# Masks and biases of attention logits: added by VectorE with the row maximum instead of by identity matmuls

## The chip, the cores and the metric

The kernel runs on one core of one Trainium2 chip. The metric is the device time of one execution in microseconds (us). Engines are named as the profile does: PE (TensorE, matmuls), PEld (its weight loads), DVE (VectorE), ACT (ScalarE), POOL (GpSimd), SP (SyncE, which issues DMAs).

## What is computed

Two transformer blocks, one after the other, on 512 tokens of width 1024, in float32. The parts that bear on the change are three attentions, each a softmax of scaled products plus a bias or a mask:

```python
def masked_softmax(logits, mask):
    logits = jnp.where(mask, logits, -jnp.inf)
    m = jnp.max(logits, axis=-1, keepdims=True)
    p = jnp.exp(logits - m)
    return p / jnp.sum(p, axis=-1, keepdims=True)
# NSA, 4 heads of 64, branches "selected" and "window": bias by distance, causal
logits_s = einsum(q_blk, kg) * scale + rel_bias[t5_bucket(dist_s)]
p_s = masked_softmax(logits_s, dist_s >= 0)
# MLA, 4 heads of 96: causal
p = masked_softmax(einsum(q_blk, k) * scale, kpos <= t0 + arange(Q_BLOCK))
# second block, grouped window attention, 8 heads: |qi - kj| <= 128, with a sink
s = jnp.where(valid, s, -jnp.inf)
m = jnp.maximum(jnp.max(s, axis=-1, keepdims=True), sk)
p = jnp.exp(s - m); p = p / (jnp.sum(p, axis=-1, keepdims=True) + jnp.exp(sk - m))
```

Around them stand projections, a compressed branch of NSA, a stick-breaking attention, a short convolution, two feed-forward nets, a gated recurrence and a cross attention to a memory.

## The kernel before

All big projections are matmuls of 128x128 weights by 512 columns, each done as three products of high and low parts (L184, L185, L186); L259 and L260 split a weight into whi (ACT) and wlo (DVE). They fill most of PE's time. The attentions work on tiles of 128 queries (NT = 4 tiles). A unit is one tile and one head (in NSA also one branch): 32 units in NSA, 16 in MLA, 32 in the window attention of the second block.

Each unit is made by `attend` in three steps. The first makes logits in a PSUM bank "L" (two of them), takes the negated row maximum (L814, DVE) and the exponential (L818, ACT, which reads the bank, takes the maximum as bias and sums the row), into an SBUF tile "sba" or "wp" (three of each). The second transposes that tile (L823, PE) and copies the result to SBUF, by ACT (L827) and DVE (L829) in turn. The third multiplies by the values (L834). `pipeline_g` runs them staggered: the second step of a unit comes two units after its first, the third three or four after. Between steps `fill` takes pieces of projection matmuls out of a list. The framework then orders each engine's queue from this program order and its own costs.

Logits are products of high and low parts: two matmuls by `mm_pair` (L879, L880) in NSA and the window attention, three (L184 to L186 with output L) in MLA. Bias and mask come on top by further matmuls into the same bank, with the identity as weights: in NSA L1124 and L1125 (high and low part of a bias table of 256 columns, tiles sbLh and sbLl, at the last 256 columns), in MLA L1337 (causal mask, 128 columns), in the window attention L1666 (upper mask at the first 128 columns, for tiles i > 0) and L1668 (causal at the last 128, for i < 3). In the window attention a `bound` lowers the negated maximum to the negated sink (L1675, DVE). NSA's compressed branch adds its bias table Tc on DVE (L1082).

The bias tables are built once: a DMA brings shifted rows, and `split` makes a high part (ACT) and a low part (DVE, L193) of their reversed columns.

Of the kernel before, what the change touches and what calls it, by code (L numbers as in the profile page):

```python
# [16 lines left out]
OP = mybir.AluOpType  # L17
# [132 lines left out]
class Kern:  # L150
# [336 lines left out]
    def setup(self):  # L487
        nc, tc, ctx, A = self.nc, self.tc, self.ctx, self.A
        self.cp = cp = ctx.enter_context(tc.tile_pool(name="cp", bufs=1))
        self.xp = ctx.enter_context(tc.tile_pool(name="xp", bufs=1))  # L490
        self.sp = ctx.enter_context(tc.tile_pool(name="sp", bufs=2))
        self.wp = ctx.enter_context(tc.tile_pool(name="wp", bufs=3))
        self.hp = ctx.enter_context(tc.tile_pool(name="hp", bufs=1))
        self.mmp = ctx.enter_context(tc.tile_pool(name="mmp", bufs=1, space=PSUM))
        self.drp = ctx.enter_context(tc.tile_pool(name="drp", bufs=1, space=DRAM))
        nc.scalar.preload_act_table_set("natural_log_exp_and_others")
        nv = A["vecs"].shape[1]
        self.vecs = self.T(cp, [P, nv], F32, "vecs")
        cm = self.T(cp, [P, P + 256], F32, "cmat")
        self.ident = cm[:, 0:P]  # L500
        self.rope = cm[:, P:P + 256].rearrange("p (t c) -> p t c", t=NT)
        self.ones = self.T(cp, [P, P], F32, "ones")
        self.mhalf = self.T(cp, [P, 12], F32, "mhalf")
        cr = self.T(cp, [P, 5 * P], F32R, "cmatr")
        nc.sync.dma_start(cm[:, :P], A["cmat"][:, :P])
        nc.vector.memset(self.ones, 1.0)
        nc.vector.memset(self.mhalf, -0.5)
        self.identr, self.trir, self.negr, self.causr, self.causupr = [cr[:, i * P:(i + 1) * P] for i in range(5)]

        def rest():  # L510
            st = self.T(self.sp, [P, 4 * P], F32, "R", 2)
            nc.sync.dma_start(st, A["cmat"][:, P:5 * P])
            nc.sync.dma_start(cm[:, P:], A["cmat"][:, 5 * P:])
            nc.vector.tensor_copy(cr[:, :P], self.ident)
            nc.vector.tensor_copy(cr[:, P:], st)

            self.lb = []
            for dr in range(2):
                l = self.T(cp, [P, 4], F32, f"lb{dr}")
                nc.vector.tensor_sub(l, self.vec(f"lb{dr}1"), self.vec(f"lb{dr}0"))  # L520
                nc.scalar.activation(l, l, AF.Exp)
                nc.vector.tensor_scalar(l, l, 1.0, None, op0=OP.add)
# [280 lines left out]
        return self.T(pool, [P, 256], F32, "junk", 1)  # L803


    def attend(self, pool, logits, nk, v, o, s, tags=("sba", "sbe", "pT"), bound=None, done=None):

        nc = self.nc
        st = {}

        def first():
            L = logits()
            nm = self.T(pool, [P, 1], F32, tags[0] + "m", 6)
            nc.vector.tensor_reduce(nm, L[:, :nk], axis=AX.X, op=OP.max, negate=True)  # L814
            if bound is not None:
                nm = bound(nm)
            p = st["p"] = self.T(pool, [P, 512], F32, tags[0], 3)
            nc.scalar.activation(p[:, :nk], L[:, :nk], AF.Exp, bias=nm, accum_out=s())  # L818
# [193 lines left out]
    def nsa_prep(self, mp, qN, kvN):  # L1012
# [17 lines left out]
        for hp in range(2):  # L1030
            Tf = self.T(mp, [P, 2, 256], F32, "sba", 3)
            nc.sync.dma_start(Tf, bass.AP(scr.tensor, scr.offset + hp * 2 * OHN + 1, [[1, P], [OHN, 2], [1, 256]]))
            tb = self.hl(mp, [P, 2, 256], "sbL", 3)
            self.split(tb, bass.AP(Tf.tensor, Tf.offset + 255, [Tf.ap[0], [256, 2], [-1, 256]]))
            TB += [tb[:, 0], tb[:, 1]]
            for i in range(NT):
                n0, n1 = max(0, 8 * i - 8), min(30, 8 * i + 6)
                s0 = n0 - (8 * i - 8)
# [4 lines left out]
                    nc.gpsimd.memset(Tc[:, i, 2 * hp:2 * hp + 2, :n0], 0.0)  # L1043
        kview = kvN[:, :, 0:256].rearrange("p t (b c) -> p t b c", b=2)[:, :, :, 0:64]
        wq = self.T(mp, [P, 1], F32, "wq8", 1)
        nc.vector.tensor_scalar(wq, self.vec("nsaq"), 0.125, None, op0=OP.mult)
        qT = []
        for c in range(2):
            self.fill(1)
# [11 lines left out]
    def nsa_units(self, mp, qts, kvN, prep, out):  # L1061
# [8 lines left out]
        def tile_units(qt):  # L1070
# [4 lines left out]
            def c_first():  # L1075
# [6 lines left out]
                nc.vector.tensor_add(lc, Lc[:, :P].rearrange("p (h n) -> p h n", n=32), Tc[:, qt])  # L1082
# [34 lines left out]
            def logits(br, h):  # L1117
                L = self.ps('L')
                self.mm_pair(L[:, :nk], h, qT, qs, kT[br], slice(0, nk))
                if qt == 0:  # L1120
                    Lb, tb = L[:, 0:P], TB[h][:, P:256]
                else:
                    Lb, tb = L[:, nk - 256:nk], TB[h]
                nc.tensor.matmul(Lb, self.identr, tb.hi, start=False, stop=True, skip_group_check=True)  # L1124
                nc.tensor.matmul(Lb, self.identr, tb.lo, start=False, stop=True, skip_group_check=True)  # L1125
                return L

            def done():
# [13 lines left out]
            for br in range(2):  # L1142
                for h in range(4):
                    vo = 64 + br * 128
                    units.append(self.attend(mp, lambda br=br, h=h: logits(br, h), nk,
                                             lambda t, vo=vo: kvN[:, t, vo:vo + 64], lambda br=br, h=h: o(br, h),
                                             lambda br=br, h=h: s(br, h), done=done if (br, h) == (1, 3) else None))
# [123 lines left out]
    def mla_proj(self, mp, ncv, cq, out):  # L1271
# [15 lines left out]
        nc.vector.tensor_scalar(wq, self.vec("mq"), 96.0 ** -0.5, None, op0=OP.mult)  # L1287
        out["mla"] = qN, kN, vN, wq

    def mla_rope(self, mp, ncv, m):  # L1290
# [34 lines left out]
    def mla_units(self, mp, hd, prep, yN):  # L1325
        nc = self.nc
        units = []

        def head(h):
            st = {}  # L1330

            def logits(qt):
# [1 line left out]
                qT, kT = hd[h]  # L1334
                L = self.ps("L")
                self.mm3(L[:, :nk], qT[:96, qt * P:nk], kT[:96, 0:nk])
                nc.tensor.matmul(L[:, nk - P:nk], self.identr, self.causr, start=False, stop=True, skip_group_check=True)  # L1337
                return L

            def o(qt):  # L1340
# [13 lines left out]
                                     rc.unsqueeze(2).to_broadcast([P, NT, 64]))  # L1354
            for qt in range(NT):
                units.append(self.attend(mp, lambda qt=qt: logits(qt), (qt + 1) * P, lambda t: prep["mla"][2][:, t, h, :],
                                         lambda qt=qt: o(qt), lambda qt=qt: s(qt), ("sba", "sbe", "pT"),
                                         done=done if qt == NT - 1 else None))
        for h in range(4):
            head(h)  # L1360
# [267 lines left out]
    def window(self, wp, qkv):  # L1628
# [15 lines left out]
        nc.vector.memset(eighth, 0.125)  # L1644
# [12 lines left out]
        def tile_units(i):  # L1657
# [4 lines left out]
            def logits(h):  # L1662
                L = self.ps('L')
                self.mm_pair(L[:, :nk], h, qT, slice(i * P, (i + 1) * P), kT[h // 4], slice(k0 * P, k1 * P))
                if i > 0:
                    nc.tensor.matmul(L[:, 0:P], self.identr, self.causupr, start=False, stop=True, skip_group_check=True)  # L1666
                if i < NT - 1:
                    nc.tensor.matmul(L[:, nk - P:nk], self.identr, self.causr, start=False, stop=True, skip_group_check=True)  # L1668
                return L

            def bound(h, m):
                if "s" not in st:
                    st["s"] = self.T(wp, [P, 8], F32, "wsum", 2)
                    st["nm"] = self.T(wp, [P, 8], F32, "wnm", 2)
                nc.vector.tensor_scalar(st["nm"][:, h:h + 1], m, nsnk[:, h:h + 1], None, op0=OP.min)  # L1675
                return st["nm"][:, h:h + 1]

            def o(h):
                if "o" not in st:
# [279 lines left out]
```

## Time and profile before

| what | us |
|---|---|
| three runs, median (lowest to highest) | 1645.45 (1644.49 to 1645.54) |
| the profiled execution, its own time | 1645.99 |
| span of its trace (1.69 lie outside) | 1644.3 |
| PE busy in the span | 1610.8 |
| DVE busy | 937.0 |
| ACT busy | 670.1 |
| POOL busy | 181.5 |

The profile is one execution. In its rows a matmul's duration runs from its start to a modelled end, and matmuls overlap, so the distance between two starts says what one takes of PE's time. [...] The first block's mixers lie before 295 us (NSA units from 138 to 240, MLA units from 255 to 290), the window attention between 950 and 1006 us.

### The profile page before, as it was taken

What the parts mean: (1) busy time and instruction counts of PE and PEld (TensorE: products, weight loads), DVE (VectorE), ACT (ScalarE), POOL (GpSimd) and SP (SyncE); (2) the same over time, 40 slices, a digit from 0 to 9 for tenths busy, and PEclk for the clock granted to TensorE, in tenths of its full rate; (3) what the DMA queues carried; (4) which work ended last, traced back from release to release, by engine and by line L of the source; (5) the groups of instructions that cost most, each with busy time, mean ns of one, the idle gap of its engine ahead of it and who ended that gap; (6) DMA issues with size and microseconds to landing.
All of it is one profiled execution on the core that took longest, in us unless ns stands there. A gap on an engine that the chain in (4) does not pass through costs nothing.

```text
span 1644.3 us, 21273 instructions
## 1 busy us (share of the span) xinstructions
PE 1610.8 (98%) x8289; PEld 1366.8 (83%) x8289; DVE 937.0 (57%) x1473; ACT 670.1 (41%) x1162; POOL 181.5 (11%) x180
## 2 busy tenths in 40 slices
PE   7999999999999999999999999999999999999998
PEld 6888888788888888878888898888888888888888
DVE  6666775644323434476766575665667556436654
ACT  4785563543222433343334354353444223223333
POOL 2121210200000001113110000330002111001110
PEclk9999999999999999999999999999999999999999
DMA  6243121133323232222222211333332333323231
GB/s 209 63 137 88 33 89 53 51 105 101 99 94 102 90 102 92 89 88 59 78 60 76 77 40 52 101 104 116 128 99 72 100 97 96 102 91 102 90 115 52
DMA packets 107976, 147.67 MB, mean 90 GB/s; under 512 B 7871, under 2 KB 58852, under 8 KB 107876
## 3 DMA queue, kind: packets, MB, share of 16 engines
q1 hardware_dynamic: 107876, 146.31, 28.3%
q8 instruction: 65, 1.06, 0.3%
q14 instruction: 35, 0.29, 0.1%
HBM read 141.79 MB, written 4.20 MB: 89 GB/s over the span
## 4 chain that ended last, share of the span: by engine, by line
PE 82%; DVE 4%; ACT 1%; DMA 1%; POOL 1%; issue 1%; SPq 0%; DVEq 0%; POOLq 0%; ACTq 0%
PE mm L184 23%; PE mm L186 23%; PE mm L185 23%; PE o L834 2%; PE lv L1560 2%; PE pT L823 1%; DVE wlo L260 1%; PE o L1603 1%; PE L L879 1%; DMA wraw<-w_down_dram 1%; PE L L880 0%; PE lv L1580 0%; POOL yq L1136 0%; DMA wraw<-w_in_dram 0%; PE L L184 0%
## 5 line engine op out<-in xcount | busy, mean ns | idle before, releaser
L260 DVE TENSOR_TENSOR wlo<-wraw,whi 128x1024 fp32r<-128x1024 f32 (+4 forms) x268 | 320.7, 1198 | 435.1 <-ACT whi L259 426.7
L259 ACT ACTIVATE whi<-wraw 128x1024 fp32r<-128x1024 f32 (+4 forms) x268 | 270.5, 1010 | 549.7 <-PE mm L185 479.8
L418 POOL TENSOR_TENSOR nacc<-nacc,nsq 128x512 f32<-128x512 f32 x30 | 46.7, 1557 | 519.6 <-ACT nsq L416 518.5
L1854 POOL TENSOR_TENSOR fz<-fz,fu 128x512 f32<-128x512 f32 x22 | 37.5, 1702 | 271.4 <-ACT fz L1853 271.4
L184 PE MATMUL mm<-H4h,whi 128*128 128x512 f32 x147 | 59.8, 407 | 0.0
L462 DVE TENSOR_TENSOR x<-mm,x 128x512 f32<-128x512 f32 x72 | 49.0, 687 | 18.7 <-PE mm L186 18.4
L184 PE MATMUL mm<-H6h,whi 128*128 128x512 f32 x147 | 58.3, 401 | 0.4 <-ACT H6h L195 0.4
L184 PE MATMUL mm<-H7h,whi 128*128 128x512 f32 x147 | 58.5, 398 | 0.0
L184 PE MATMUL mm<-H5h,whi 128*128 128x512 f32 x147 | 58.3, 396 | 0.0
L186 PE MATMUL mm<-H4h,wlo 128*128 128x512 f32 x147 | 57.5, 391 | 0.7 <-DVE wlo L260 0.7
L186 PE MATMUL mm<-H6h,wlo 128*128 128x512 f32 x147 | 57.9, 394 | 0.0
L185 PE MATMUL mm<-H6l,whi 128*128 128x512 f32 x147 | 57.8, 393 | 0.0
L186 PE MATMUL mm<-H5h,wlo 128*128 128x512 f32 x147 | 57.4, 390 | 0.0
L185 PE MATMUL mm<-H5l,whi 128*128 128x512 f32 x147 | 57.4, 390 | 0.0
L186 PE MATMUL mm<-H7h,wlo 128*128 128x512 f32 x147 | 57.4, 390 | 0.0
L185 PE MATMUL mm<-H4l,whi 128*128 128x512 f32 x147 | 57.3, 390 | 0.0
L185 PE MATMUL mm<-H7l,whi 128*128 128x512 f32 x147 | 57.3, 390 | 0.0
L184 PE MATMUL mm<-H0h,whi 128*128 128x512 f32 x139 | 55.7, 401 | 0.5 <-ACT whi L259 0.5
L184 PE MATMUL mm<-H2h,whi 128*128 128x512 f32 x139 | 55.8, 402 | 0.0
L184 PE MATMUL mm<-H3h,whi 128*128 128x512 f32 x139 | 55.7, 401 | 0.0
L184 PE MATMUL mm<-H1h,whi 128*128 128x512 f32 x139 | 55.1, 396 | 0.0
L186 PE MATMUL mm<-H3h,wlo 128*128 128x512 f32 x139 | 54.8, 394 | 0.0
(1214 smaller groups left out, 4448.5 us busy)
## 6 DMA issues: line engine op xcount, KB each, us to landing
wraw<-ffn_w_dram SPq DMA_DIRECT2D x64, 512.0 KB, 3.6
wraw<-w_up_dram SPq DMA_DIRECT2D x88, 256.0 KB, 3.1
wraw<-w_in_dram SPq DMA_DIRECT2D x36, 512.0 KB, 3.5
wraw<-w_down_dram SPq DMA_DIRECT2D x22, 512.0 KB, 3.6
wraw<-w_mem_kv_dram SPq DMA_DIRECT2D x16, 512.0 KB, 3.7
wraw<-w_in_dram SPq DMA_DIRECT2D x52, 128.0 KB, 2.3
wraw<-w_in_dram SPq DMA_DIRECT2D x20, 256.0 KB, 2.8
wraw<-cmp_w_dram SPq DMA_DIRECT2D x8, 512.0 KB, 4.2
```

Of the source, the lines that this page charges most:

```text
L184: mm(out, a.hi, b.hi, start=start, stop=False, skip_group_check=skip)
L185: mm(out, a.hi, b.lo, start=False, stop=False, skip_group_check=skip)
L186: mm(out, a.lo, b.hi, start=False, stop=stop, skip_group_check=skip)
L259: nc.scalar.activation(hi, raw, AF.Copy)
L260: nc.vector.tensor_sub(lo, raw, hi.bitcast(F32))
L418: eng.tensor_add(nm.acc, nm.acc, sq[:, :nm.N])
L462: self.nc.vector.tensor_add(self.x[k], b, self.x[k])
L823: nc.tensor.transpose(b[:, t * P:(t + 1) * P], st["p"][:, t * P:(t + 1) * P], self.ident)
L834: nc.tensor.matmul(o(), st["pT"][:, t * P:(t + 1) * P], v(t), start=(t == 0), stop=(t == nt - 1))
L879: self.nc.tensor.matmul(out, q[h][:, qs], k.hi[:, ks], start=True, stop=False)
L1560: nc.tensor.matmul(b[:, t * P:(t + 1) * P], ym[:, t * P:(t + 1) * P], mix(X, c, t * P, P), start=True, stop=True)
L1854: nc.gpsimd.tensor_mul(z, z, us[c])
```

## The change

The scale that goes into the queries changes its sign, so that the banks hold negated logits. Then one DVE instruction, `tensor_tensor_reduce`, adds a table of negated biases or masks, writes the sum to the SBUF tile and takes the minimum of the row, starting from a value `least` (the negated sink in the window attention, 3.0e38 elsewhere). ACT's exponential reads that SBUF tile with scale -1, in place. The identity matmuls go, and with them the 32 minima L1675. The tables are as wide as the longest row of logits: four tiles of 512 columns in NSA (256 of them zero), one in MLA, one of 384 in the window attention.

```diff
+        cn = self.T(cp, [P, 2 * P], F32, "cmask2")
...
+            nc.vector.tensor_scalar(cn, st[:, 2 * P:], -1.0, None, op0=OP.mult)
...
             L = logits()
-            nm = self.T(pool, [P, 1], F32, tags[0] + "m", 6)
-            nc.vector.tensor_reduce(nm, L[:, :nk], axis=AX.X, op=OP.max, negate=True)
-            if bound is not None:
-                nm = bound(nm)
+            nm, least = bound() if bound is not None else (self.T(pool, [P, 1], F32, tags[0] + "m", 6), 3.0e38)
             p = st["p"] = self.T(pool, [P, 512], F32, tags[0], 3)
-            nc.scalar.activation(p[:, :nk], L[:, :nk], AF.Exp, bias=nm, accum_out=s())
+            nc.vector.tensor_tensor_reduce(p[:, :nk], L[:, :nk], bias, 1.0, least, op0=OP.add, op1=OP.min, accum_out=nm)
+            nc.scalar.activation(p[:, :nk], p[:, :nk], AF.Exp, bias=nm, scale=-1.0, accum_out=s())
...
-            tb = self.hl(mp, [P, 2, 256], "sbL", 3)
-            self.split(tb, bass.AP(Tf.tensor, Tf.offset + 255, [Tf.ap[0], [256, 2], [-1, 256]]))
-            TB += [tb[:, 0], tb[:, 1]]
+            for a, tg in enumerate(("sbLh", "sbLl")):
+                tb = self.T(mp, [P, S], F32, tg, 3)
+                nc.gpsimd.memset(tb[:, :256], 0.0)
+                nc.scalar.activation(tb[:, 256:], bass.AP(Tf.tensor, Tf.offset + 256 * a + 255, [Tf.ap[0], [-1, 256]]),
+                                     AF.Copy, scale=-1.0)
+                TB.append(tb)
...
-        nc.vector.tensor_scalar(wq, self.vec("nsaq"), 0.125, None, op0=OP.mult)
+        nc.vector.tensor_scalar(wq, self.vec("nsaq"), -0.125, None, op0=OP.mult)
...
                 self.mm_pair(L[:, :nk], h, qT, qs, kT[br], slice(0, nk))
-                if qt == 0:
-                    Lb, tb = L[:, 0:P], TB[h][:, P:256]
-                else:
-                    Lb, tb = L[:, nk - 256:nk], TB[h]
-                nc.tensor.matmul(Lb, self.identr, tb.hi, start=False, stop=True, skip_group_check=True)
-                nc.tensor.matmul(Lb, self.identr, tb.lo, start=False, stop=True, skip_group_check=True)
                 return L
...
+        cm = self.T(mp, [P, S], F32, "sbLh", 3)
+        nc.gpsimd.memset(cm[:, :S - P], 0.0)
+        nc.gpsimd.tensor_copy(cm[:, S - P:], self.ncaus)
...
-                nc.tensor.matmul(L[:, nk - P:nk], self.identr, self.causr, start=False, stop=True, skip_group_check=True)
...
+        wb = self.T(wp, [P, 3, P], F32, "wb")
+        nc.gpsimd.tensor_copy(wb[:, 0], self.ncausup)
+        nc.gpsimd.memset(wb[:, 1], 0.0)
+        nc.gpsimd.tensor_copy(wb[:, 2], self.ncaus)
...
-                if i > 0:
-                    nc.tensor.matmul(L[:, 0:P], self.identr, self.causupr, start=False, stop=True, skip_group_check=True)
-                if i < NT - 1:
-                    nc.tensor.matmul(L[:, nk - P:nk], self.identr, self.causr, start=False, stop=True, skip_group_check=True)
...
-                nc.vector.tensor_scalar(st["nm"][:, h:h + 1], m, nsnk[:, h:h + 1], None, op0=OP.min)
-                return st["nm"][:, h:h + 1]
+                return st["nm"][:, h:h + 1], nsnk[:, h:h + 1]
```

Left out of it: the compressed branch subtracts in place of adding, the MLA and window queries get the same change of sign, and the identity is no longer cast for PE.

PE's queue in the window attention, one unit of the second tile, before (L is the bank of logits, pT and o those of the transposes and of the output; wk and wq are keys and queries, cmatr the constant matrices):

```order
L879 MATMUL L_8189<-wk1h_7899,wq2h_7862 128x384
L880 MATMUL L_8189<-wk1l_7900,wq2h_7862 128x384
L1666 MATMUL L_8189<-cmatr_80 128x128
L1668 MATMUL L_8189<-cmatr_80 128x128
L823 MATMUL pT_8202<-cmat_77,wp_8130 128x128 x3
L834 MATMUL o_8182<-qkv_6001,wpT_8180 128x64 x3
```

The same place in the changed kernel, where mm is the bank of a projection:

```order
L881 MATMUL L_8081<-wk1h_7831,wq2h_7794 128x384
L882 MATMUL L_8081<-wk1l_7832,wq2h_7794 128x384
L186 MATMUL mm_8270<-H2h_5482,wlo_8275 128x512
L881 MATMUL L_8102<-wk1h_7831,wq2l_7797 128x384
L882 MATMUL L_8102<-wk1l_7832,wq2l_7797 128x384
L825 MATMUL pT_8068<-cmat_77,wp_8008 128x128 x3
L836 MATMUL o_8074<-qkv_5929,wpT_8035 128x64 x3
L184 MATMUL mm_8270<-H3h_5496,whi_8274 128x512
L185 MATMUL mm_8270<-H3l_5497,whi_8274 128x512
L825 MATMUL pT_8090<-cmat_77,wp_8025 128x128 x3
L836 MATMUL o_8074<-qkv_5929,wpT_8072 128x64 x3
```

The rows L1666 and L1668 are gone, and pieces of a projection (L184 to L186), which before stood elsewhere in the queue, now stand between the units.

DVE's queue in the NSA units beside the MLA preparation (mss, mrr2t and mrr2u belong to that preparation, wlo to a weight), before:

```order
L814 TENSOR_REDUCE sbam_2393<-L_2388 128x1
L210 TENSOR_SCALAR mrr2t_2309<-mss_527_2283 128x32
L814 TENSOR_REDUCE sbam_2414<-L_2409 128x1
L196 SCALAR_TENSOR_TENSOR mla_t_2794<-yT_445_1996,vecs_76,mla_p_2793 128x512
L217 TENSOR_TENSOR mrr2u_2311<-mrr_536_2308 128x32
L196 SCALAR_TENSOR_TENSOR mla_t_2796<-yT_447_2003,vecs_76,mla_p_2795 128x512
L218 TENSOR_TENSOR mrr2u_2311<-mrr2u_2311,mrr2t_2309 128x32
L814 TENSOR_REDUCE sbam_2435<-L_2430 128x1
```

And in the changed kernel, where the two rows L819 are one `tensor_tensor_reduce`, and the second of them only writes the row's minimum:

```order
L831 COPY sbe_2333<-pT_2329 128x384
L210 TENSOR_SCALAR mrr2t_2274<-mss_528_2248 128x32
L260 TENSOR_TENSOR wlo_2344<-wraw_2342,whi_2343 128x512
L819 ISA sba_2355,sbam_2354<-L_2351,sbLl_1289 128x384
L819 ISA sbam_2354 128x1
L819 ISA sba_2374,sbam_2373<-L_2370,sbLh_1300 128x384
L819 ISA sbam_2373 128x1
L217 TENSOR_TENSOR mrr2u_2276<-mrr_537_2273 128x32
L260 TENSOR_TENSOR wlo_2398<-wraw_2396,whi_2397 128x512
```

Each maximum L814 has become two rows, of which the first also reads a bias table (sbLh, sbLl) and writes the tile sba.

## Rows read from the trace of the kernel before

**Rows 1.** page, busy time of each engine and the chain that ended last
```profile
PE 1610.8 (98%) x8289; PEld 1366.8 (83%) x8289; DVE 937.0 (57%) x1473; ACT 670.1 (41%) x1162; POOL 181.5 (11%) x180
PE 82%; DVE 4%; ACT 1%; DMA 1%; POOL 1%; issue 1%; SPq 0%; DVEq 0%; POOLq 0%; ACTq 0%
```

**Rows 2.** by stage: stretch, length, busy PE, PEld, DVE, ACT, POOL (instructions), clock, DMA
```profile
138.00:180.00 42.00, 39.81 (x239) 33.36 (x238) 23.09 (x67) 19.62 (x69) 4.95 (x5) 1.00 0.14 40
180.00:217.00 37.00, 36.03 (x236) 31.79 (x234) 35.30 (x103) 24.09 (x64) 5.28 (x8) 1.00 0.20 58
255.00:290.00 35.00, 34.12 (x222) 30.16 (x220) 20.86 (x42) 15.58 (x44) 1.02 (x2) 1.00 0.20 61
966.00:990.00 24.00, 24.00 (x202) 23.78 (x201) 16.61 (x46) 14.13 (x42) 0.00 (x0) 1.00 0.01 2
```

**Rows 3.** lines L1124 and L1668: count, shortest/median/longest ns, first and last start
```profile
L1124 PE MATMUL L<-sbLh,cmatr x32: 274/279/415, 140.5 to 238.4; 128*128 128x256 f32 x24, 128*128 128x128 f32 x8
L1668 PE MATMUL L<-cmatr x24: 221/276/279, 952.9 to 987.3; 128*128 128x128 f32 x24
```

**Rows 4.** timeline of PE in an NSA unit: start us, us, engine, line, tiles
```profile
174.02 0.28 PE L1124 MATMUL L<-sbLh,cmatr 128*128 128x256 f32 x1
174.14 0.28 PE L1125 MATMUL L<-sbLl,cmatr 128*128 128x256 f32 x1
```

**Rows 5.** by stage, 180 to 217: first L1124 (PE, PEld), then L814 (DVE) alone
```profile
180.00:217.00 37.00, 2.88 (x10) 1.88 (x10) 1.00 0.20 58
180.00:217.00 37.00, 5.84 (x11) 1.00 0.20 58
```

**Rows 6.** timeline of PE in two MLA units
```profile
260.23 0.23 PE L1337 MATMUL L<-cmatr 128*128 128x128 f32 x1
260.29 0.38 PE L823 MATMUL pT<-cmat,sba 128*128 128x128 f32 x2
261.50 0.27 PE L1337 MATMUL L<-cmatr 128*128 128x128 f32 x1
261.61 0.48 PE L184 MATMUL mm<-mla_p,whi 128*128 128x512 f32 x1
```

**Rows 7.** timeline of all engines in one unit of the window attention
```profile
976.35 0.23 PE L1666 MATMUL L<-cmatr 128*128 128x128 f32 x1
976.41 0.28 PE L1668 MATMUL L<-cmatr 128*128 128x128 f32 x1
976.52 0.52 PE L823 MATMUL pT<-cmat,wp 128*128 128x128 f32 x3
976.72 0.56 DVE L814 TENSOR_REDUCE wpm<-L 128x1 f32<-128x384 f32 x1 [0.20 <-PE L L1668]
977.62 0.58 ACT L818 ACTIVATE wp<-L,wnm 128x384 f32<-128x384 f32 x1
977.89 0.23 PE L1666 MATMUL L<-cmatr 128*128 128x128 f32 x1
```

**Rows 8.** groups of DVE by shape (columns as in the page); last, line L1644
```profile
L814 DVE TENSOR_REDUCE sbam<-L 128x1 f32<-128x512 f32 x12 | 8.2, 686 | 4.6 <-PE L L1337 4.6
L462 DVE TENSOR_TENSOR x<-mm,x 128x512 f32<-128x512 f32 x72 | 49.0, 687 | 18.7 <-PE mm L186 18.4
L1675 DVE TENSOR_SCALAR wnm<-wpm,nsnk 128x1 f32<-128x1 f32 x32 | 6.7, 210 | 0.5
L1644 DVE MEMSET w<- x1: 59/59/59, 928.5 to 928.5; 128x1 f32 x1
```

**Rows 9.** groups of ACT by shape, copies of 512 columns from SBUF and PSUM
```profile
L192 ACT ACTIVATE sbLh<-sbe 128x512 fp32r<-128x512 f32 x8 | 5.0, 630 | 2.1 <-POOL sbe L896 1.4 <-DVE rnf L755 0.7
L192 ACT ACTIVATE mpTh<-pt 128x512 fp32r<-128x512 f32 x8 | 4.8, 597 | 3.8 <-PE pt L1782 3.8
```

**Rows 10.** waits of PE, 135 to 295: us in total, times, longest
```profile
PE mm L427 <- POOL nacc L977: 1.2, 1, 1.2
```

**Rows 11.** by stage, one microsecond in NSA's last tile
```profile
230.00:231.00 1.00, 1.00 (x6) 1.00 (x6) 0.80 (x1) 0.62 (x2) 1.00 (x1) 0.50 0.00 0
```

More of the change, by code (lines that the diff above doesn't have):

```diff
@@ L503, in setup @@
         self.mhalf = self.T(cp, [P, 12], F32, "mhalf")
-        cr = self.T(cp, [P, 5 * P], F32R, "cmatr")
+        cr = self.T(cp, [P, 2 * P], F32R, "cmatr")
+        cn = self.T(cp, [P, 2 * P], F32, "cmask2")
         nc.sync.dma_start(cm[:, :P], A["cmat"][:, :P])
@@ L507, in setup @@
         nc.vector.memset(self.mhalf, -0.5)
-        self.identr, self.trir, self.negr, self.causr, self.causupr = [cr[:, i * P:(i + 1) * P] for i in range(5)]
+        self.trir, self.negr = [cr[:, i * P:(i + 1) * P] for i in range(2)]
+        self.ncaus, self.ncausup = [cn[:, i * P:(i + 1) * P] for i in range(2)]
         def rest():
@@ L513, in rest @@
             nc.sync.dma_start(cm[:, P:], A["cmat"][:, 5 * P:])
-            nc.vector.tensor_copy(cr[:, :P], self.ident)
-            nc.vector.tensor_copy(cr[:, P:], st)
+            nc.vector.tensor_copy(cr, st[:, :2 * P])
+            nc.vector.tensor_scalar(cn, st[:, 2 * P:], -1.0, None, op0=OP.mult)
             self.lb = []
@@ L803, in junk, with attend @@
         return self.T(pool, [P, 256], F32, "junk", 1)
-    def attend(self, pool, logits, nk, v, o, s, tags=("sba", "sbe", "pT"), bound=None, done=None):
+    def attend(self, pool, logits, nk, v, o, s, bias, tags=("sba", "sbe", "pT"), bound=None, done=None):
         nc = self.nc
@@ L1081, in c_first @@
                 lc = st["lc"] = self.T(mp, [P, 4, 32], F32, "nlc", 1)
-                nc.vector.tensor_add(lc, Lc[:, :P].rearrange("p (h n) -> p h n", n=32), Tc[:, qt])
+                nc.vector.tensor_sub(lc, Tc[:, qt], Lc[:, :P].rearrange("p (h n) -> p h n", n=32))
                 mc = self.T(mp, [P, 4], F32, "nmc", 2)
@@ L1146, in tile_units @@
                                              lambda t, vo=vo: kvN[:, t, vo:vo + 64], lambda br=br, h=h: o(br, h),
-                                             lambda br=br, h=h: s(br, h), done=done if (br, h) == (1, 3) else None))
+                                             lambda br=br, h=h: s(br, h), TB[h][:, S - nk:],
+                                             done=done if (br, h) == (1, 3) else None))
             units.insert(first + 3, (nop, c_second, c_third))
@@ L1286, in mla_proj @@
         wq = self.T(mp, [P, 1], F32, "mwq", 1)
-        nc.vector.tensor_scalar(wq, self.vec("mq"), 96.0 ** -0.5, None, op0=OP.mult)
+        nc.vector.tensor_scalar(wq, self.vec("mq"), -96.0 ** -0.5, None, op0=OP.mult)
         out["mla"] = qN, kN, vN, wq
@@ L1356, in head @@
                 units.append(self.attend(mp, lambda qt=qt: logits(qt), (qt + 1) * P, lambda t: prep["mla"][2][:, t, h, :],
-                                         lambda qt=qt: o(qt), lambda qt=qt: s(qt), ("sba", "sbe", "pT"),
+                                         lambda qt=qt: o(qt), lambda qt=qt: s(qt), cm[:, S - (qt + 1) * P:],
                                          done=done if qt == NT - 1 else None))
@@ L1643, in window @@
         eighth = self.T(wp, [P, 1], F32, "w8")
-        nc.vector.memset(eighth, 0.125)
+        nc.vector.memset(eighth, -0.125)
+        wb = self.T(wp, [P, 3, P], F32, "wb")
+        nc.gpsimd.tensor_copy(wb[:, 0], self.ncausup)
+        nc.gpsimd.memset(wb[:, 1], 0.0)
+        nc.gpsimd.tensor_copy(wb[:, 2], self.ncaus)
+        wb = wb.rearrange("p a n -> p (a n)")
         qT = []
@@ L1664, in logits, with bound @@
                 self.mm_pair(L[:, :nk], h, qT, slice(i * P, (i + 1) * P), kT[h // 4], slice(k0 * P, k1 * P))
-                if i > 0:
-                    nc.tensor.matmul(L[:, 0:P], self.identr, self.causupr, start=False, stop=True, skip_group_check=True)
-                if i < NT - 1:
-                    nc.tensor.matmul(L[:, nk - P:nk], self.identr, self.causr, start=False, stop=True, skip_group_check=True)
                 return L
-            def bound(h, m):
+            def bound(h):
                 if "s" not in st:
@@ L1695, in tile_units @@
                                          lambda t, kh=kh: qkv[:, k0 + t, 640 + kh * 64:704 + kh * 64],
-                                         lambda h=h: o(h), lambda h=h: st["s"][:, h:h + 1], ("wp", "wpT", "pT"),
-                                         bound=lambda m, h=h: bound(h, m), done=done if h == 7 else None))
+                                         lambda h=h: o(h), lambda h=h: st["s"][:, h:h + 1],
+                                         wb[:, P if i == 0 else 0:(P if i == 0 else 0) + nk], ("wp", "wpT", "pT"),
+                                         bound=lambda h=h: bound(h), done=done if h == 7 else None))
         for i in range(NT):
```

## The prediction

> **What bounds the kernel now.** I read the page first, then its chain of waits, then a table by stage, then single lines. The page: PE is busy 1610.8 us of 1644.3, DVE 937.0, and 82% of the chain that ended last is PE [rows 1]. So what counts is PE time, but only in stretches where nothing else is late. The table by stage gives these stretches [rows 2]. From 138 to 180 us (first NSA units) DVE is busy 23.09 of 42.00 us; from 255 to 290 (MLA) 20.86 of 35.00; from 966 to 990 (the middle of the window attention) 16.61 of 24.00 while PE is busy all 24.00. In these the reader is to see a full PE and a DVE with room. From 180 to 217 (later NSA units, with the short convolution and the MLA preparation beside them) DVE is busy 35.30 of 37.00: there two engines are full at once, and work taken from PE and put on DVE may bring nothing.
>
> **Part 1: 128 matmuls go.** The diff removes 32 of L1124 [rows 3], as many of L1125 (both always run), 16 of L1337 (four heads by four tiles), 24 of L1668 [rows 3], and 24 of L1666 (three of four tiles, eight heads, as L1668). The 276 and 279 ns of such rows are not the price: matmuls overlap, so the price is the distance from one start to the next.
> - NSA: 174.02 to 174.14 is 0.12 us for one [rows 4]. L1124 runs 10 times between 180 and 217 us [rows 5], so 20 of the 64 matmuls lie in the stretch where DVE is full and 44 outside. Outside: 44 x 0.12 = 5.3 us off PE. Inside: 20 x 0.12 = 2.4 us off PE, of which I count nothing, since the 1.7 us that DVE idles there (37.00 less 35.30) leaves it last in line.
> - MLA: 0.06 us before a transpose (260.23 to 260.29) and 0.11 before a projection (261.50 to 261.61) [rows 6]. At the mean, 16 x 0.08 = 1.3 us.
> - Window: L1666 takes 976.35 to 976.41, L1668 976.41 to 976.52 [rows 7]. 24 x 0.06 + 24 x 0.11 = 4.1 us. One unit takes 1.54 us (976.35 to 977.89), and would take 1.54 - 0.17 = 1.37.
>
> Sum off PE where it counts: 5.3 + 1.3 + 4.1 = 10.7 us; with the 2.4 also, 13.1 us.
>
> **Part 2: DVE does sum and minimum in one.** 80 maxima (L814) become 80 fused instructions. No row of before shows a fused one. Lower end: it costs what the maximum alone costs, 686 ns at 512 columns [rows 8], because an addition of a PSUM and an SBUF operand of that size, L462, takes 687 ns too: both look bound by columns, not by what is done to each. Upper end: the two it replaces one after the other, twice the row. I take the lower end, since an instruction with two operands stands at 687 and one with one at 686, so a second operand is free in this size. Below the maximum's own cost it can't come, since it reads the same columns and writes them too. Order shows each as two instructions, the second only writing the 128x1 result. Bounds for that: 59 ns, the memset of one column (L1644), and 210 ns, L1675, which reads and writes one column [rows 8]. It reads nothing from memory, which is nearer the memset; overlapped with its neighbours I take 0.11 us. In the full stretch 11 units run [rows 5]: 11 x 0.11 = 1.2 us that DVE has to find there (0.6 to 2.3 by the ends). I count it in full as loss. Elsewhere it is hidden: in the window stage DVE has 24.00 - 16.61 = 7.39 us idle in some 15 units, 0.5 us each; the reads add 0.11 and the 32 L1675 go, so DVE gets no busier. If that cover were gone each window unit would lose 0.1 us, 3 us in all.
>
> [...]
>
> **Part 3: the exponential reads SBUF.** ScalarE's copies of 512 columns take 597 ns from PSUM and 630 from SBUF [rows 9]; so some 33 ns more each, 80 x 0.03 = 2.6 us on an engine that is busy 670.1 us of 1644.3 [rows 1]. Cover: the transposes of a unit stand two units behind its logits, in the window stage 3 us, while its maximum, sink and exponential take 976.72 to 978.20 [rows 7], 1.5 us. At nothing. The PSUM bank of the logits is now free after DVE instead of after ScalarE, earlier by 0.6 us. What PE waits for that bank could come back; all of ScalarE's share of the chain that ended last is 1% of the span [rows 1], with every other wait for ScalarE in it, so I take nothing, and leave a gain of 1 us to the lower part of the range.
>
> **Part 4: the tables.** Four bias tiles are made by four ScalarE copies and four POOL memsets instead of a split into a high and a low part, and two mask tiles by POOL. DVE loses two subtractions, POOL gains about ten small instructions; POOL is busy 181.5 us in all [rows 1]. All are made during setup or projections, where PE has matmuls queued. The fifth load of w_out moves behind eight reloads of x on SP's queue; it is not the next weight that PE takes. Nothing for each; if a POOL piece came late, under 1 us.
>
> **Sum.** 1645.99 (the profiled execution) - 10.7 + 1.2 = 1636.5 us; that execution is 0.5 above the median of 1645.45, so **1636** beside the median.
>
> **The rivals.**
> - *All PE time counts, and a clock dip goes.* DVE finds its 1.2 us, its order lets PE run on in the full stretch, 13.1 us come off, and one spell at half clock goes. [...] 1645.5 - 13.1 - 1.5 = 1631. For it: order interleaves more projection matmuls into the units. [...]
> - *The reordered queues open new gaps.* The program between units is scheduled anew on every engine; the softmax of a unit is a chain PE, DVE, ScalarE, PE. If it becomes longer than two units where few projections lie between (MLA, the last NSA tile), PE waits 0.3 us at some 15 units, and one more spell at half clock costs 1.5: 4.5 + 1.5 of 9.5 gone, 1642. For it: just such waits stand in before, if few. Against: the chain gets only the read and 33 ns longer.
> - *The fused instruction costs both that it replaces: slower.* Place: DVE in the full NSA stretch and the window stage. Price: in the stretch the 5.84 us of maxima [rows 5] come a second time, 7.0 with the reads, against 1.7 idle: 5.3 lost. In the window, DVE needs 16.61/24.00 x 1.54 = 1.07 us a unit, and with 0.56 more [rows 7] 1.63, so it and no longer PE sets the unit: 0.09 over the 1.54 of before, 32 x 0.09 = 2.9 lost. Against that, 5.3 + 1.3 gained elsewhere: 1.6 lost, and one more dip of the clock 1.5: 1645.5 + 3.1 = 1649. It decides from 0.47 us extra per window unit, where DVE reaches 1.54. Against: the rows of equal length. [...]
> - *The change doesn't do what it says.* Order shows no identity matmul left on PE; what remains is that the freed time was never on the path: 1645. Against it the window stage, where PE is busy 24.00 of 24.00.
>
> **How the numbers follow.** Main forecast 0.52 (its own range 1634 to 1638.5, from the ends of the read and the 2.4 us); all PE time 0.15; new gaps 0.20, half of it over 0.2% faster and half within; fused at double 0.10; no effect 0.03. A measurement of this kernel can tell about 0.2%, 3.3 us, from no change. Faster by more: 0.52 + 0.15 + 0.10 = 0.77; within: 0.10 + 0.03 = 0.13; slower: 0.10. The range 1631 to 1645 leaves out the slower case and a tail at either end, under 0.2.
>
> **What would show it.** Right: no idle PE in the window stage, one unit in about 1.37 us; fused rows of 0.55 at 384 columns and 0.69 at 512; the second instruction near 0.1; DVE over 95% busy between 180 and 215. Wrong: fused rows above 0.8 us at 384, PE waiting for DVE or ScalarE before transposes, new stretches at granted clock 0.50.

## The result, and the profile after

The changed kernel takes 1632.32 us (median of 4, 1631.53 to 1634.0) against 1645.49 beside it: ratio 0.9922, 95% interval 0.991 to 0.9935. That is 13.2 us faster; 9.5 were forecast. The time lies below the main forecast's own range (1634 to 1638.5) and inside the whole one (1631 to 1645), near its lower end. Two more sets of runs of the same kernel gave 1633.13 and 1632.19.

About one of the 13.2 us is the clock. The granted clock (the column behind POOL in a table by stage) is the share of its full speed that TensorE got: at 1.00 projection matmuls of 512 columns start 0.23 us apart (before, 300.53 and 300.76), at 0.50 they start 0.42 apart (the changed kernel, 181.49 and 181.91). Runs whose mean granted clock was the same can be compared: at 0.996 the kernel before took 1644.2 us (mean of 10 runs) and the changed one 1632.2 (5 runs), at 0.995 they took 1645.1 (14) and 1633.6 (4). So 11.5 to 12.0 us remain at equal clock.

The page of the changed kernel, its busy times and the chain that ended last, against [rows 1]:

```profile
PE 1594.7 (98%) x8161; PEld 1347.4 (83%) x8161; DVE 931.9 (57%) x1519; ACT 671.0 (41%) x1164; POOL 182.1 (11%) x189
PE 88%; DVE 5%; issue 3%; ACT 1%; POOL 1%; DMA 1%; SPq 0%; DVEq 0%; POOLq 0%; ACTq 0%
```

PE is busy 16.1 us less (durations overlap and their ends are modelled, so this is not the time gained), DVE 5.1 us less in spite of 46 more instructions, ScalarE 0.9 more. The stages of [rows 2] in the changed kernel, same columns; the stretches are set earlier, by what had been gained up to them:

```profile
138.00:176.50 38.50, 37.09 (x216) 30.66 (x215) 23.11 (x81) 20.43 (x70) 4.96 (x5) 1.00 0.15 43
176.50:213.00 36.50, 34.30 (x202) 29.46 (x200) 32.18 (x108) 22.58 (x60) 5.72 (x8) 0.95 0.20 59
250.00:284.00 34.00, 33.01 (x210) 28.81 (x208) 20.79 (x58) 16.29 (x45) 1.13 (x2) 1.00 0.12 40
958.00:979.00 21.00, 21.00 (x162) 19.78 (x161) 12.67 (x40) 12.38 (x37) 0.00 (x0) 1.00 0.00 1
```

The second row is the stretch where DVE was busy 35.30 of 37.00 us; now 32.18 of 36.50, so it did not fill up. A spell at half clock lies in this stretch (clock 0.95) and gives DVE time; in the kernel's second trace (e8), which has none there, DVE is busy 33.84 of the 37.00 us from 174 on, 91%. The last row shows the window attention with PE busy all of it, as before.

DVE's groups of the fused instruction, by shape (columns as in [rows 8]):

```profile
L819 DVE CUSTOM_DVE_ANT_0 wp<-L,wb,nsnk 128x384 f32<-128x384 f32 x16 | 9.8, 613 | 3.6 <-PE pT L825 3.4
L819 DVE CUSTOM_DVE_ANT_0 sba<-L,sbLh 128x512 f32<-128x512 f32 x8 | 5.5, 682 | 4.1 <-PE L L186 4.1
L819 DVE CUSTOM_DVE_ANT_0 sba<-L,sbLh 128x384 f32<-128x384 f32 x8 | 4.4, 555 | 2.7 <-PE L L186 2.5 <-PE L L882 0.2
L819 DVE DVE_READ_ACCUMULATOR2_ANT sbam<- 128x1 f32 x48 | 4.0, 83 | 0.0
```

512 columns take 682 ns, the 686 of the maximum alone [rows 8]. In the window attention 384 columns take 613, against 557 for the maximum alone there and 210 for the L1675 that is gone. The second instruction takes 83 ns, between the two bounds. Whether it takes a place in the queue is in DVE's timeline of the changed kernel (first three rows) and of before (last two, a second fence):

```profile
217.62 0.68 DVE L819 CUSTOM_DVE_ANT_0 sba<-L,sbLl 128x512 f32<-128x512 f32 x1
218.23 0.09 DVE L819 DVE_READ_ACCUMULATOR2_ANT sbam<- 128x1 f32 x1
218.23 0.17 DVE L1095 TENSOR_SCALAR nsc<-nsc 128x4 f32<-128x4 f32 x1
```

```profile
219.60 0.69 DVE L814 TENSOR_REDUCE sbam<-L 128x1 f32<-128x512 f32 x1
220.20 0.28 DVE L1089 TENSOR_REDUCE nsc<-nlc 128x4 f32<-128x128 f32 x1
```

The read and the instruction behind it start at the same time, 218.23, and that is 0.61 us after the fused one; the maximum alone held DVE for 0.60. Here the read costs nothing. In 38 of the 80 reads of this trace the next instruction starts together with the read; behind nearly all others DVE idles first.

**Where the time comes from.** The same matmul can be looked up in two traces, and the difference of its starts is PE's lead over before. PE's timeline, six projection matmuls in before:

```profile
138.03 0.33 PE L185 MATMUL mm<-wlo,H7h 128*128 128x364 f32 x1
...
179.02 0.40 PE L186 MATMUL mm<-H7h,wlo 128*128 128x512 f32 x1
...
245.96 0.40 PE L185 MATMUL mm<-mla_t,whi 128*128 128x512 f32 x1
...
307.59 0.39 PE L184 MATMUL mm<-H5h,whi 128*128 128x512 f32 x1
...
947.20 0.39 PE L185 MATMUL mm<-rT3l,whi 128*128 128x512 f32 x1
...
1016.77 0.39 PE L186 MATMUL mm<-H0h,wlo 128*128 128x512 f32 x1
```

and the same six in the changed kernel:

```profile
138.29 0.33 PE L185 MATMUL mm<-wlo,H7h 128*128 128x364 f32 x1
...
174.88 0.48 PE L186 MATMUL mm<-H7h,wlo 128*128 128x512 f32 x1
...
240.78 0.39 PE L185 MATMUL mm<-mla_t,whi 128*128 128x512 f32 x1
...
300.50 0.39 PE L184 MATMUL mm<-H5h,whi 128*128 128x512 f32 x1
...
938.84 0.39 PE L185 MATMUL mm<-rT3l,whi 128*128 128x512 f32 x1
...
1003.69 0.39 PE L186 MATMUL mm<-H0h,wlo 128*128 128x512 f32 x1
```

The lead goes from -0.26 to 5.18 over the NSA units (4.14 of it by 179 us, where the stretch with the full DVE begins), to 7.09 over MLA, to 8.36 by 947 and to 13.08 over the window attention: 5.4, 1.9, 1.3 and 4.7 us.

The 1.3 us from 307 to 947 come nearly all at one place, 718 to 721 us, where no line of the change runs: before has a spell at half clock there (3.4 us at a granted clock of 0.50) and the changed kernel has none, though PE waits 2.2 us just ahead of that place in both. So spells have to be taken out of such sums. A short spell loses 1.7 us: from 181 on the rows of the changed kernel, one for each microsecond, read 0.70, 0.50, 0.50, 0.60, which is 0.3 + 0.5 + 0.5 + 0.4. Between 138 and 246 us before lost 1.7 us to spells and the changed kernel 3.4, since it has a new one behind a new wait of 1.0 us (below). At equal clock, if each spell costs all that it loses, the NSA units gave 5.4 + 1.7 = 7.1 us. No spell lies between 138 and 179 us in either trace: 4.4 came there, and the other 2.7 behind.

### The profile page after: what moved, and what is told of

It is laid out like the page before. It is cut to its first block, busy times and chain, and to the rows that moved or that the text cites. A ratio compares the mean times of both kernels' runs of the same rounds, so it can differ in the third digit from the quotient of the medians.

```text
span 1630.1 us, 21078 instructions
## 1 busy us (share of the span) xinstructions
PE 1594.7 (98%) x8161; PEld 1347.4 (83%) x8161; DVE 931.9 (57%) x1519; ACT 671.0 (41%) x1164; POOL 182.1 (11%) x189
## 4 chain that ended last, share of the span: by engine, by line
PE 88%; DVE 5%; issue 3%; ACT 1%; POOL 1%; DMA 1%; SPq 0%; DVEq 0%; POOLq 0%; ACTq 0%
PE mm L184 25%; PE mm L186 25%; PE mm L185 25%; PE o L836 2%; PE lv L1562 2%; DVE wlo L260 1%; PE pT L825 1%; PE o L1605 1%; PE L L881 1%; PE L L882 0%; PE o L938 0%; ACT whi L259 0%; PE lv L1582 0%; DVE x L462 0%; PE o L427 0%
## 5 line engine op out<-in xcount | busy, mean ns | idle before, releaser
L184 PE MATMUL mm<-H4h,whi 128*128 128x512 f32 x147 | 59.5, 405 | 0.0
L186 PE MATMUL mm<-H4h,wlo 128*128 128x512 f32 x147 | 57.6, 392 | 0.7 <-DVE wlo L260 0.7
L184 PE MATMUL mm<-H7h,whi 128*128 128x512 f32 x147 | 58.1, 396 | 0.0
L184 PE MATMUL mm<-H5h,whi 128*128 128x512 f32 x147 | 58.1, 395 | 0.0
L184 PE MATMUL mm<-H6h,whi 128*128 128x512 f32 x147 | 57.5, 394 | 0.4 <-ACT H6h L195 0.4
L186 PE MATMUL mm<-H6h,wlo 128*128 128x512 f32 x147 | 57.5, 391 | 0.0
L186 PE MATMUL mm<-H7h,wlo 128*128 128x512 f32 x147 | 57.4, 390 | 0.0
L186 PE MATMUL mm<-H5h,wlo 128*128 128x512 f32 x147 | 57.3, 390 | 0.0
L184 PE MATMUL mm<-H0h,whi 128*128 128x512 f32 x139 | 55.6, 400 | 0.5 <-ACT whi L259 0.5
L184 PE MATMUL mm<-H2h,whi 128*128 128x512 f32 x139 | 55.5, 399 | 0.0
L184 PE MATMUL mm<-H3h,whi 128*128 128x512 f32 x139 | 55.4, 398 | 0.0
L184 PE MATMUL mm<-H1h,whi 128*128 128x512 f32 x139 | 55.0, 396 | 0.0
L186 PE MATMUL mm<-H3h,wlo 128*128 128x512 f32 x139 | 54.8, 394 | 0.0
```

Source lines behind the costliest of these rows:

```text
L184: mm(out, a.hi, b.hi, start=start, stop=False, skip_group_check=skip)
L186: mm(out, a.lo, b.hi, start=False, stop=stop, skip_group_check=skip)
```

## The experiments

The same matmuls give each kernel's lead by stage (us gained on the first trace of before; "clock" is what the NSA stage lost to spells, 1.7 in before; the last column is the NSA gain with that difference taken out):

| kernel | median us | NSA | MLA | window | clock | NSA at equal clock |
|---|---|---|---|---|---|---|
| changed | 1632.32 | 5.4 | 1.9 | 4.7 | 3.4 | 7.1 |
| changed again (e8) | 1633.13 | 6.7 | 1.9 | 4.8 | 1.7 | 6.7 |
| changed once more (e10) | 1632.19 | 5.5 | 1.9 | 4.7 | 3.4 | 7.2 |
| e1, no identity matmuls | 1635.29 | 2.4 | 1.5 | 5.0 | 5.1 | 5.8 |
| e2, fused, matmuls kept | 1641.93 | 2.5 | 1.8 | -0.8 | 0.0 | 0.8 |
| e9, bank held | 1635.29 | 1.6 | 2.6 | 5.1 | 5.1 | 5.0 |
| before again (e12) | 1645.39 | -1.6 | 0.5 | 0.0 | 3.4 | 0.1 |

### Each half of the change alone (e1, e2)

e1 takes the identity matmuls of all three attentions out of before (two of them shown), and so leaves out the biases and masks; e2 puts as many, on a tile of zeros, into the changed kernel:

```diff
-                nc.tensor.matmul(Lb, self.identr, tb.hi, start=False, stop=True, skip_group_check=True)
-                nc.tensor.matmul(Lb, self.identr, tb.lo, start=False, stop=True, skip_group_check=True)
...
```

```diff
+                nc.tensor.matmul(Lb, self.identr, self.zr[:, :w], start=False, stop=True, skip_group_check=True)
+                nc.tensor.matmul(Lb, self.identr, self.zr[:, :w], start=False, stop=True, skip_group_check=True)
...
```

> The kernel before without its 128 identity matmuls; biases and masks of the NSA, MLA and window units are left out, everything else is as before (maximum alone on VectorE, exponential from PSUM, L1675 kept). Theory A, the gain of the change is TensorE time and nothing else: 1645.5 - 13 = about 1632, like the changed kernel, with TensorE's lead over before built up by about 7 us in the NSA units, 1.2 in MLA and 4.7 in the window attention. Theory B, a part of it comes from the other edits (the PSUM bank free after VectorE, no L1675, the tables): 1635 to 1638, and the window attention gains under 4. If the accumulator reads cost the full NSA stretch 1.2 us in the changed kernel, this one is that much faster there: 1630 to 1631.

> The changed kernel, with as many matmuls of the same shapes put back behind the logits, multiplying a tile of zeros: the VectorE side of the change alone. Theory A: what was gained is lost again, 1645 to 1646.5, the upper end if the reads and the longer exponential cost something; no lead in the window attention. Theory B: 1640 to 1643, since the other edits keep their part.

Measured: e1 1635.29 (ratio 0.9938, 0.9923 to 0.9953), 10.1 us under before's 1645.41; e2 1641.93 (0.9987, 0.9974 to 1.0), between no gain and 4 us. So theory A falls: the matmuls alone give 10.1 of the 13.2, and the rest needs the fused instruction as well. Alone, the fused instruction gives 1.8 us in MLA and little elsewhere: e2's trace has no spell in the NSA units, so at equal clock its gain there is 0.8 us, and in the window attention it loses 0.8, which stays unexplained. e1 also says where its gain comes from. In the window attention it gains 5.0 us, more than the changed kernel; there PE time is all. In the NSA units it gains less, and the waits of PE there show why (line waited for: us in total, times, longest), e1 from 135 to 300 us:

```profile
PE mm L427 <- POOL nacc L977: 2.0, 1, 2.0
...
PE L L1079 <- ACT sba L818: 1.6, 1, 1.6
PE L L184 <- ACT sba L818: 1.2, 1, 1.2
PE L L879 <- ACT sba L818: 0.9, 1, 0.9
```

the changed kernel, same stretch:

```profile
PE pT L825 <- DVE sbe L831: 1.5, 2, 1.2
PE mm L427 <- POOL nacc L979: 1.2, 1, 1.2
PE pT L1108 <- DVE sbe L831: 1.2, 1, 1.2
PE L L1084 <- DVE sbam L819: 1.0, 1, 1.0
PE L L184 <- DVE sbam L819: 0.7, 1, 0.7
...
PE L L881 <- DVE sbam L819: 0.2, 1, 0.2
```

and before:

```profile
PE L L184 <- ACT sba L818: 0.7, 1, 0.7
PE L L879 <- ACT sba L818: 0.6, 1, 0.6
```

The rows with output L are waits for a bank of logits, 1.3 us in before. With the matmuls gone PE comes to the bank earlier and stands before it 3.7 us; with the fused instruction, which lets go of the bank after DVE instead of after ScalarE, 1.9.

### The bank held until the exponential is done (e9)

```diff
+            nc.scalar.activation(self.T(pool, [P, 1], F32, "hold", 2), L[:, :1], AF.Copy)
```

> The changed kernel with one more ScalarE copy of a single column from the logits' PSUM bank behind each exponential, so that the bank comes free only after ScalarE, as in before; 80 copies. Theory E: with the matmuls gone TensorE comes to the bank earlier, and the earlier release is what keeps its waits at 1.9 us in the NSA and MLA units (1.0, 0.7 and 0.2 on the minimum of VectorE), against 3.7 without the fused instruction (1.6, 1.2 and 0.9 on the exponential of ScalarE). Held, these waits rise to 4 us or more and the time to 1634.5 to 1637. Theory D, what lies between the two is the clock's chance: waits may move, the time stays at 1632 to 1633. The window attention should keep its lead of 4.7 us.

Measured: 1635.29 (0.9943, 0.9931 to 0.9955), 3.1 us over the changed kernel beside it (e10, 1632.19). The waits of PE between 135 and 305 us:

```profile
PE mm L427 <- POOL nacc L980: 2.0, 1, 2.0
PE pT L826 <- ACT hold L821: 1.7, 1, 1.7
PE L L1085 <- ACT hold L821: 1.6, 1, 1.6
PE L L882 <- ACT hold L821: 1.3, 2, 1.0
...
PE L L184 <- ACT hold L821: 0.3, 1, 0.3
```

The bank's waits rise from 1.9 to 3.2 us, less than the 4 expected. The wait before transposes at 147 us, now for an added copy, grows from 1.2 to 1.7, and L427 waits 2.0 us as in e1, with a spell behind it that is twice as long (5.1 against 3.4 us lost in the NSA units). All waits of PE in this stretch add up to 9.6 us, against 8.1 in the changed kernel. The window attention keeps its lead, as expected. The time is that of e1. So the earlier release is worth at most what separates e1 from the changed kernel, about 3 us, 1.7 of it time at half clock by the traces. The edit also puts 80 small copies on ScalarE (the 1.7 us wait is one of these), and which part of the 3.1 is theirs was not tried.

### A second pass on VectorE (e3)

```diff
+            nc.vector.tensor_reduce(self.T(pool, [P, 1], F32, "dbl", 2), p[:, :nk], axis=AX.X, op=OP.min)
             nc.scalar.activation(p[:, :nk], p[:, :nk], AF.Exp, bias=nm, scale=-1.0, accum_out=s())
```

> The changed kernel with one more VectorE reduction over the same row between the fused instruction and the exponential, 80 of them: what the rival of the prediction priced, a fused instruction that costs both that it replaces. By the prediction's rival about 5 us lost in the full NSA stretch and 7 in the window attention, the rest of the gain kept: 1632.3 + 12 = 1644 (without the dip of the clock that the rival added). If VectorE has more room than its busy share says: 1634 to 1637, and the loss only in NSA.

Measured: 1647.5 (1.0013, 1.0001 to 1.0024): 15 us over the changed kernel, and 2 over before. The slower rival was priced right in sum, 1649, but not in its places. PE's waits in the NSA and MLA units, 135 to 320 us, grew:

```profile
PE mm L186 <- DVE wlo L260: 2.5, 1, 2.5
PE pT L826 <- ACT sba L821: 1.6, 1, 1.6
PE L L882 <- DVE sbam L819: 1.6, 2, 1.4
```

PE lost 3.7 us of lead in each of NSA and MLA instead of gaining 5.4 and 1.9, much of it to spells at half clock: there are four in that stretch, one of some 7 and one of some 10 us, and together they lose 12 us, where the changed kernel's two lose 3.4. In the window attention it still gained 4.7 (read at a matmul far behind it, at 1500.95 us in before). A stretch of that stage, PE full and DVE with room, columns as in [rows 2]:

```profile
960.00:985.00 25.00, 25.00 (x165) 21.90 (x164) 19.20 (x58) 14.85 (x40) 0.26 (x1) 1.00 0.14 43
```

The rival counted durations, 1.63 us of DVE a unit. But an instruction's duration reaches past the start of the next one: by starts a fused one of 384 columns takes 0.54 in e3 (0.61 long) and the copy or reduction of as many some 0.47 (0.55 long), so a unit (with a copy of its transposes on DVE in every second one) needs an estimated 0.54 + 0.47 + half of 0.47 = 1.25 us, under PE's 1.36.

### The tables on VectorE (e4, e11)

```diff
-                nc.gpsimd.memset(tb[:, :256], 0.0)
+                nc.vector.memset(tb[:, :256], 0.0)
...
-        nc.gpsimd.memset(cm[:, :S - P], 0.0)
-        nc.gpsimd.tensor_copy(cm[:, S - P:], self.ncaus)
+        nc.vector.memset(cm[:, :S - P], 0.0)
+        nc.vector.tensor_copy(cm[:, S - P:], self.ncaus)
```

> The changed kernel with the four zero fills of the bias tables, and the fill and copy of the MLA mask, on VectorE instead of POOL. In the trace of the changed kernel they stand between the last mask operations of the stick-breaking attention at 111.8 to 112.6 us, and TensorE loses 0.9 us of its lead at 113 to 115. If POOL's queue is the cause: the lead stays at +0.7 there, and the time is 0.9 lower, about 1631.4. If it is something else that the new order brings: no change, 1632.3.

> The tables on VectorE once more, with five rounds. If the 0.9 us of lead that TensorE keeps at 113 to 115 us reach the end: 1631.5, 0.9 below the changed kernel of the same chip. If a later wait takes them: 1632.4.

The reason is in POOL's timeline of the changed kernel: three pieces of table stand between the mask operations (L898) of the stick-breaking attention,

```profile
111.04 0.79 POOL L898 TENSOR_SCALAR_AFFINE_SELECT sba<-sba 128x128 f32<-128x128 f32 x1 [1.16 <-ACT sba L930]
111.78 0.31 POOL L1037 MEMSET sbLl<- 128x256 f32 x1
112.03 0.41 POOL L1329 MEMSET sbLh<- 128x384 f32 x1
112.40 0.28 POOL L1330 COPY sbLh<-cmask 128x128 f32<-128x128 f32 x1
112.64 0.74 POOL L898 TENSOR_SCALAR_AFFINE_SELECT sba<-sba 128x128 f32<-128x128 f32 x1
```

and PE's lead falls from +0.66 to -0.26 there. In e4 and e11 it doesn't fall (0.49 and 0.49; -1.20 and -1.21). Measured: e4 1631.98 and e11 1632.95, against 1632.32 and 1632.19 (e10) for the changed kernel. So the cause is shown, and its worth at the end is not: 0.9 us is less than these runs tell apart.

> The changed kernel once more, beside e9 and e11 on the same chip, with five rounds: 1632.4, and a wait of 0.9 us at about 113 to 115 us.

### POOL's queue behind the convolution (e5, e6, e7)

```diff
-            nc.gpsimd.tensor_mul(y, y, t)
+            (nc.vector if c else nc.gpsimd).tensor_mul(y, y, t)
...
-                nc.gpsimd.tensor_add(acc, acc, sq)
+                nc.vector.tensor_add(acc, acc, sq)
```

> The kernel before, with one edit of another kind: the last two elementwise operations of the short convolution (L970 for the second channel half, L977) run on VectorE instead of POOL. In before POOL runs two additions of the NSA output (L1136, 1.5 us) ahead of L970 and then L977, and TensorE waits 1.2 us for L977 (L427), after which the clock falls to 0.50 for 3.5 us. Theory C, the part of the gain that TensorE time does not explain (13.2 against 10.1 with the matmuls alone taken away) is this queue: before gains 1.5 to 3 us from the edit, 1642.5 to 1644, with the wait of L427 under 0.3 us. Theory D, the part is the clock's chance: 1645.4, no gain.

> The same edit on the kernel without identity matmuls (biases and masks of the NSA, MLA and window units left out). There TensorE waits 2.0 us for L977 and runs 7.5 us at 0.50. Theory C: it comes down by 3 us to the changed kernel's time, 1632, or below. Theory D: 1635.3 as before the edit.

> The changed kernel with the tables on VectorE and the same convolution edit. In the changed kernel POOL runs L972 ahead of the additions of the NSA output, but one of them still stands ahead of L979, and TensorE waits 1.2 us. Theory C: 1 to 3 us below 1632.0, so 1629 to 1631. Theory D, or VectorE too full there: 1632.

Measured: before with the edit 1639.75 against 1646.67 (0.996, 0.9945 to 0.9975), without identity matmuls 1634.8, the changed kernel with both edits 1632.06. In all three the wait of L427 for POOL is gone. In e6 PE waits elsewhere instead, from 215 to 250 us:

```profile
PE pT L823 <- ACT sba L818: 1.3, 1, 1.3
```

and in e6 and e7 the time stays. Theory C falls as an explanation of the gain: removing that wait brings e1 no nearer to the changed kernel. What e5 gained is more than the wait: its trace has no spell at half clock before the very end; before has four, at 29, 230, 295 and 718 us. Those at 29 and 718 lie where the edit changes nothing, so a good part of its 6.9 us is the clock. Why stays open.

### The same kernels once more (e8, e12)

> The changed kernel as it is, once more, to see which spells at half clock come back at the same place. If they follow from TensorE's own waits, the ones at 181 and 226 us stand there again and the ones that before has at 294 and 718 us do not: 1632.3. If they are chance, the places differ and the time moves by 1.7 us a spell: 1630 to 1635.

> The kernel before, as it is, for a second trace: 1645.5. If its spells at half clock follow from TensorE's waits they stand again at 29, 230, 294 and 718 us; what differs between the two traces of the same kernel is the chance that any comparison of two traces carries.

Measured: 1633.13 and 1645.39. Nearly all waits of PE are the same to 0.1 us in the traces of one kernel; the spells are not. Microsecond 182 of the changed kernel, first trace and second:

```profile
182.00:183.00 1.00, 1.00 (x5) 0.80 (x4) 0.97 (x3) 0.00 (x0) 0.00 (x0) 0.50 0.03 8
```

```profile
182.00:183.00 1.00, 1.00 (x7) 0.92 (x6) 1.00 (x5) 1.00 (x6) 0.00 (x0) 1.00 0.02 6
```

and microsecond 295 of before, first and second:

```profile
295.00:296.00 1.00, 1.00 (x4) 0.81 (x3) 0.58 (x2) 1.00 (x4) 0.00 (x0) 0.50 0.00 0
```

```profile
295.00:296.00 1.00, 0.70 (x7) 0.51 (x6) 0.37 (x1) 0.26 (x1) 0.00 (x0) 1.00 0.00 0
```

The wait of 1.0 us at 179 stands in both traces of the changed kernel, the spell behind it in one. In before's second trace PE did not slow down at 295 and idled instead (busy 0.70), and it came out of there 0.5 us ahead of the first, so that spell had cost 0.5 us and not 1.7.

## Why the prediction was right, and where not

- **What bounds the kernel:** right. PE time came off where PE was full and DVE had room. The window attention's unit was forecast at 1.37 us; in the changed kernel's timeline of PE the transposes of two units in a row start 1.36 apart where no piece of a projection stands between them (1.46 to 1.94 in the units beside them, which have such pieces):

```profile
967.45 0.49 PE L825 MATMUL pT<-cmat,wp 128*128 128x128 f32 x3
...
968.81 0.49 PE L825 MATMUL pT<-cmat,wp 128*128 128x128 f32 x3
```

- **Part 1, the matmuls:** 10.7 us of PE time where it counts, and e1 measured 10.1; the two agree in sum more than in their places. Window: 4.1 forecast, 4.7 to 5.0 measured. The 0.11 for L1668 was read in a middle tile; in the eight units of the first tile the next matmul starts 0.06 later, and over all 48 matmuls these distances add up to 3.7, so about 1 us of this gain has another source, which stays open. MLA: 1.3 and 1.9, of which 0.5 is the spell at 295; e2, which keeps the matmuls, gains 1.8 there too, so this gain is not shown to be theirs. NSA was the term that was mis-sized: 5.3 less 1.2 of Part 2, 4.1 in all, against 6.7 to 7.2 at equal clock. Up to 179 us 28 of its matmuls go, 3.4 us by the step's price, and 4.4 were gained. From there on the sum has 16 x 0.12 = 1.9 less 1.2, 0.7 us, and 2.4 to 2.9 were gained at equal clock in three traces. So the step that failed is the one that counted nothing for the stretch where DVE was full. I took DVE's busy share for its limit. Busy time counts an instruction to its end, but the next one can start some 0.09 us earlier (0.69 us long, 0.60 from start to start), so DVE had more room than 37.00 less 35.30.
- **Part 2, the fused instruction:** the lower end was right in NSA and MLA (682 and 555 ns); in the window attention it took 56 ns more than the maximum alone. The 1.2 us for reading the result was not lost: 83 ns each, and where DVE goes straight on, the next instruction starts together with the read (38 of 80) or before its end (2); behind the other 40 DVE idles first. With the 2.4 us that I counted nothing for, the sum was 3.6 us too low behind 179 us, and 1.7 to 2.2 of these were measured; e2 shows no loss in the NSA units either.
- **Part 3:** the longer exponential cost nothing visible (718 ns at 512 columns, 684 before). The earlier release of the bank, counted at nothing with 1 us left to the range, is worth up to 3.1 us (e9), time at half clock and the cost of the added copies included. The step went by ScalarE's 1% of before's chain; it should have asked what before's waits for the bank, 1.3 us, become when PE arrives earlier: 3.7 us in e1.
- **Part 4:** POOL's pieces did come late, 0.9 us, within the 1 us that the step allowed.
- **The rivals:** "all PE time counts, and a clock dip goes", 1631, came nearest, and its sum of 13.1 us of PE time is close to the gain by stage. No run shows the 1.5 us that this and the next two rivals take for a spell at half clock: the spell of before at 230 reads 0.94, 0.50, 0.50, 0.50, 0.85 by microsecond from 229, a loss of 1.7, and the one at 295 cost 0.5. The dip of the first rival is chance: the changed kernel got a spell at 181 in its first trace and lost others. New gaps did open (L1084, 1.0 us, and L825 and L1108, 1.2 each) while others closed: from 135 to 305 us PE's waits add up to 8.1 us, against 6.6 in before. The slower rival's sum held in e3 (1647.5 against 1649), but by luck: the loss lies in NSA and MLA alone, and much of it is time at half clock; the fused instruction itself does not cost that much (682 ns, against 686 for the maximum alone).
- **The signs named:** DVE was not over 95% busy in the full stretch but 88% (91% in the trace without a spell there), which is the failed step again. The fused row of 384 columns read 555 in NSA and 613 in the window attention, neither above 0.8.

## What to carry to other kernels

An addition to a PSUM operand that a DVE reduction has to read anyway can be free when it is fused into it (682 ns against 686 here, and 56 ns more in the form with a start value in SBUF), and matmuls that only add a table were then worth about their start-to-start distance where PE was the full engine (0.06 to 0.12 us each here, 10.7 us forecast from them and 10.1 measured in e1). When PE work goes, look next at the buffers that PE will reach earlier: a bank let go one engine sooner was worth up to a quarter of this gain (3.1 of 13.2 us, e9). For DVE as for PE, take distances between starts, not durations or busy shares, before calling it full (0.60 us from start to start against 0.69 of duration for a maximum of 512 columns; 0.23 against 0.39 for a matmul of 512, before at 300.53).

## What the runs showed of the hardware

- The read of DVE's accumulator lasts 83 ns, and in 38 of 80 cases the next instruction starts together with it (the changed kernel's first trace).
- The fused instruction took 613 ns in the window attention and 555 in NSA for the same 384 columns (479 and 419 for 256). The forms differ in the start value, a column of SBUF there and a constant here; that this is the cause was not tried.
- Half-clock spells mostly stand behind a wait of PE of 0.9 to 3.1 us, but the wait does not decide it: the one of 2.2 us at 716 us in before is in all 14 traces, and a spell stands behind it in 7; the spell at 295 in before has only waits of 0.2 to 0.4 us ahead of it. A short spell (3.4 us at a granted clock of 0.50) loses 1.7 us at most (at 295 in before it cost 0.5), and the runs of one kernel spread over 2 to 7 us. A difference of 1 us between two kernels needs more runs than these.
